# Hybrid decoder trunk: the attention branch by seven products of halves, gated straight from PSUM

## The chip, the cores and the metric

The kernel runs on one core of a Trainium2 chip. TensorE (PE) multiplies matrices into PSUM; VectorE (DVE), ScalarE (ACT) and GpSimd (POOL) work on tiles in the core's memory; SyncE (SP) and POOL issue transfers (DMA). Each engine works through its own instructions in program order, and semaphores make it wait for others. The metric is the device time of one execution in microseconds (us), the median of several.

## The reference

Two layers; each adds a feed-forward block, a mixer of two gated branches, and another feed-forward block to x (512 tokens of 1024 features, f32). What the change touches is in the mixer:

```python
h = rmsnorm(x, ln_mix[l])
z = h @ w_in[l]
u_pool, q, k, v, gate_logits = jnp.split(z, splits, axis=-1)
a = pool_mixer(u_pool, pool_w[l], pool_scale[l]) @ w_pool_branch[l]
...
b = swa_sink_attention(q, k, v, sinks[l]) @ w_attn_branch[l]
g_pool, g_attn = jnp.split(jax.nn.sigmoid(gate_logits), N_BRANCHES, axis=-1)
x = x + (g_pool * a + g_attn * b) @ w_out[l]
```

The attention's output has 512 features (8 heads of 64), both branches' products give 1024, and `w_out` is 1024 x 1024.

## The kernel before

**Products.** Operands are f32 values kept as a high part (a cast by ACT to the type that PE multiplies fast) and a remainder (what DVE subtracts: `lo = src - hi`); a product is three matmuls, high by high, high by remainder, remainder by high. Almost all matrix products go by Winograd's form of Strassen's scheme (`strassen`, line 556): instead of eight products of halves there are seven, named `a11, s1, s2, a12, s3, s4, a22`, whose operands are sums of halves and whose results are added up in PSUM and afterwards. With four blocks of weights, each has up to two chunks of 128x1024 and each chunk takes twelve matmuls of 128x512.

**Weights.** `Weights` (line 178) keeps a plan of chunks in the order of their use. SP loads a chunk into one of seven buffers `raw` (`issue`, line 253); for s1 and s3, whose weights are sums, POOL then issues a transfer that adds the other half onto it (`more`). The sums of s2 and s4 are made by DVE (`add_up`, line 264, into `sums`), or, in blocks called `moved`, that of s4 by one more adding transfer by POOL as soon as the sum of s2 was split (`then`, at the end of `low`). ACT casts the chunk to `wh` (four buffers), DVE takes the remainder `wl` (three). `prep` (line 319), called once per chunk used, does one more step of each; a load waits until the buffer seven chunks earlier has had its last use.

**The mixer** (`mix`, line 920). In the order of PE's program: queries, keys and values; two blocks of gates (`gates`), in whose 28 pieces `side` (line 1150) places the attention, the normalisation and the pooling step by step after tables of slots (`HEADS`, `ATT`, `POOL`); the pool branch (line 1331, `branch` in four quarters of 24 matmuls, with the slots from 28 on beside it); the attention branch, four more quarters, also by `branch`; then the product with `w_out` by the class `Down` (line 597), seven products of two chunks.

The result of a gate is a tile of 128x1024 for each half (i = 0, 1 of the features) and each branch: `z[i]["r"]` and `["u"]` receive the pool branch times its gate (two halves of the tokens, r and u), `z[i]["d"]` and `["p"]` hold the attention's gate. A quarter of the attention branch is evacuated by two DVE operations, the gate times PSUM into `d` or `p`, and that added to `r` or `u`. PE then transposes the four finished tiles (`dn.turned`, eight transposes of 128x128 into the only tile of that kind, `pt`, which ACT and DVE must have emptied before the next group), and from `pt` ACT and DVE make the operands `op` of `Down` and its sums `fa`, `fb`, `fc`. In the rows below `zr_3585` and `zu_3712` are z0's r and u, `zr_4062` and `zu_4204` those of z1; a number is that of the tile.

The attention's output `pv` is written to two tiles per step, `ah` by ACT and `al` by DVE, and the pooling's weights come by one 256 KB transfer `praw`, issued on SP's queue in slot 15 of the gates and split in slot 17.

The first two lines below are the two that decide when a transfer may go and when a weight sum is made; the rest is the evacuation of a quarter of the attention branch.

```python
self.loaded < RAW or self.loads[self.loaded - RAW]["uses"] == 0
if self.summed >= upto + 2 * (c["kind"] == "s2"):
...
nc.vector.tensor_tensor(out=v, in0=pt, in1=v, op=ALU.mult)
add(y, y, v)
```

Of the kernel before, what the change touches and what calls it, by code (L numbers as in the profile page):

```python
# [19 lines left out]
P = 128  # L20
# [95 lines left out]
def trunk(ctx, tc, x0, xT, consts, vecs, rows, w_g4, w_g3, w_d8, w_d6, w_kv, w_uq, w_pool, w_gate, w_br, w_out, out):  # L116
# [61 lines left out]
    class Weights:  # L178
# [3 lines left out]
        def __init__(self):  # L182
# [41 lines left out]
        def block(self, w, sizes, order, start=False, between=(), moved=False):  # L224
# [3 lines left out]
                   "a22": ((1, 1), None), "s2": (None, None), "s4": (None, None)}  # L228
            for k in order:
                for c in range(2):  # L230
# [4 lines left out]
            for c in range(2):  # L235
# [8 lines left out]
            get = lambda *kinds: [name[k, c] for k in kinds for c in range(2)]  # L244
# [311 lines left out]
    def strassen(roles, order, n, sizes, operand, steps, mid={}):  # L556
        A, C, Dd = roles if len(roles) > 2 else (*roles, roles[1])
        bank = {"a11": A, "s2": A, "s3": A, "a22": A, "s1": C, "s4": C, "a12": Dd}
        for kind in order:
            pt, first = bank[kind], kind in ("a11", "s1", "a12") or kind == "s4" and C is Dd  # L560
            k0 = 0
            for c, kn in enumerate(sizes):
                wh, wl = (t[:, :kn * n].rearrange("p (k f) -> p k f", k=kn) for t in W.take(kind))
                for q in range(2):
                    for k in range(kn):
                        ah, al = operand(kind, k0 + k, q)
                        for j, (s, m) in enumerate(((ah, wh), (ah, wl), (al, wh))):
# [10 lines left out]
                if c == 0:  # L578
# [18 lines left out]
    class Down:  # L597


        def __init__(self, turn, op_of, f_of, aside_of, coef, nxt, last=False):  # L600
# [14 lines left out]
            def turned(src, i, t, n):  # L615
# [7 lines left out]
                if i == 0 and t == 1:  # L623
# [24 lines left out]
            def down(n, final, roles, more={}):  # L648
# [71 lines left out]
                }  # L720
                mid.update(more)
# [198 lines left out]
    def mix(ctx, l, nm, nxt):  # L920
# [20 lines left out]
        us = up.tile([P, len(WIN), S], F32, name="us")  # L941
        qT, tiles, parts_, out = {}, {}, {}, {}
# [33 lines left out]

        def pool_weights():
            praw = temp("praw")
# [83 lines left out]
        def attend(b, jp):  # L1062
# [67 lines left out]
            if "ah" not in out:  # L1130
                out.update((t, ap.tile([P, 4, S], F32R, name=t, tag=t)) for t in ("ah", "al"))
# [14 lines left out]
        for g, at in zip(work, [(1, 2), (15, 17), *HEADS, *ATT, *POOL]):  # L1146
            for t in at:
                beside.setdefault(t, []).append(g)

        def side(t):  # L1150
            for g in beside.pop(t, ()):
                next(g)
# [166 lines left out]
        todo = [(i, k) for i in range(2) for k in ("r", "u")] + [(i, k) for i in range(2) for k in ("p", "d")]  # L1319
# [6 lines left out]
        at = 28  # L1326
        for i in range(2):
# [16 lines left out]
        opened(len(todo))  # L1344
        assert not beside, beside
        banks.close()
        order_[:] = order_[1], order_[0], order_[2]
# [7 lines left out]
        def op_of(name):  # L1355
# [4 lines left out]
        spare = up.tile([P, 4, S], F32, name="aside", tag="us")  # L1360
        dn = Down(
            turn, op_of, lambda name: z_tile("f" + name, dict(b="p", a="d", c="u")[name]),
            lambda i: spare[:, 2 * i:2 * i + 2, :], 1.0, nxt,
        )
        for i in range(2):
# [131 lines left out]
```

## Time and profile before

| what | us |
|---|---|
| median of 3 runs (lowest, highest) | 1823.79 (1823.51, 1824.49) |
| the profiled execution in all | 1827.11 |
| its span | 1825.1 |
| busy DVE, ACT in the span | 1512.7, 1133.7 |
| layer 0: attention branch, first to last matmul | 517.59 to 541.14 |

The profiled execution is one more than the three runs, and times of instructions are from it. A row of the timeline reads: start, length, engine, line (here always that of a helper through which every instruction goes, L93 before and L98 after), operation, result <- operands, their sizes; in brackets the idle time of the engine before it and what ended it. Matmuls are pipelined, so the cost of one is the distance of two starts and not its length. A row on waits reads: who waited <- for whom: us in total, times, longest. A row of transfers has the queue, the number, the size and the median time in us from issue to landing.

### The profile page before, as it was taken

What the parts mean: (1) busy time and instruction counts of PE and PEld (TensorE: products, weight loads), DVE (VectorE), ACT (ScalarE), POOL (GpSimd) and SP (SyncE); (2) the same over time, 40 slices, a digit from 0 to 9 for tenths busy, and PEclk for the clock granted to TensorE, in tenths of its full rate; (3) what the DMA queues carried; (4) which work ended last, traced back from release to release, by engine and by line L of the source; (5) the groups of instructions that cost most, each with busy time, mean ns of one, the idle gap of its engine ahead of it and who ended that gap; (6) DMA issues with size and microseconds to landing.
All of it is one profiled execution on the core that took longest, in us unless ns stands there. A gap on an engine that the chain in (4) does not pass through costs nothing.

```text
span 1825.1 us, 24191 instructions
## 1 busy us (share of the span) xinstructions
PE 1815.0 (99%) x8828; PEld 1531.7 (84%) x8828; DVE 1512.7 (83%) x1828; ACT 1133.7 (62%) x1635; POOL 192.5 (11%) x220
## 2 busy tenths in 40 slices
PE   9999999999999999999999999999999999999998
PEld 9988888887788889988888898888867888899887
DVE  8877878889869987887998878788987798878877
ACT  6655555767847754655765555567777477556554
POOL 0100101110001110110100111101100011111000
PEclk9999999999999999999999999999999999999999
DMA  8887867677436867797767779777764368767864
GB/s 258 205 239 182 225 171 188 180 197 192 133 99 160 221 174 193 181 248 181 192 170 205 172 182 235 197 195 177 215 161 123 104 162 207 193 168 193 239 181 127
DMA packets 103831, 338.90 MB, mean 186 GB/s; under 512 B 11264, under 2 KB 11520, under 8 KB 103712
## 3 DMA queue, kind: packets, MB, share of 16 engines
q1 hardware_dynamic: 69408, 231.80, 37.4%
q0 software_dynamic: 34160, 105.53, 33.8%
q8 instruction: 69, 1.13, 0.3%
q14 instruction: 50, 0.41, 0.1%
q10 hardware_dynamic: 144, 0.03, 0.0%
HBM read 320.54 MB, written 2.10 MB: 177 GB/s over the span
## 4 chain that ended last, share of the span: by engine, by line
PE 95%; DVE 3%; ACT 1%; DMA 1%; issue 0%; DVEq 0%; ACTq 0%; SPq 0%
PE mm L93 89%; PE pt L93 3%; DVE wl L93 1%; PE pt_pv L93 1%; PE pt_tp L93 1%; DMA praw<-in_w_pool 1%; DVE more L93 0%; DVE sums L93 0%; ACT wh L93 0%; ACT xg L93 0%; PE cold L93 0%; ACT p L93 0%; DVE xg L93 0%; DVE win L93 0%; DVE m L93 0%
## 5 line engine op out<-in xcount | busy, mean ns | idle before, releaser
L93 PE MATMUL mm<-wh,xg 128*128 128x512 f32 (+2 forms) x2032 | 613.7, 373 | 0.9 <-ACT xg L93 0.8
L93 DVE TENSOR_TENSOR wl<-raw,wh 128x1024 fp32r<-128x1024 f32 (+3 forms) x459 | 524.4, 1148 | 98.1 <-PE mm L93 76.2
L93 ACT CAST wh<-raw 128x1024 fp32r<-128x1024 f32 (+3 forms) x459 | 451.2, 991 | 201.9 <-PE mm L93 122.6
L93 PE MATMUL mm<-wh,more 128*128 128x512 f32 (+1 forms) x1520 | 472.9, 380 | 0.0
L93 PE MATMUL mm<-wh,op 128*128 128x512 f32 x1456 | 465.1, 394 | 0.0
L93 PEld LDWEIGHTS mm<-wh,xg 128*128 128x128 f32 x2032 | 375.4, 188 | 59.0 <-ACT xg L93 2.1
L93 PE MATMUL mm<-wl,xg 128*128 128x512 f32 (+2 forms) x1016 | 376.2, 370 | 0.2 <-DVE wl L93 0.2
L93 PEld LDWEIGHTS mm<-wh,more 128*128 128x128 f32 x1520 | 283.5, 188 | 51.3 <-issue 4.6
L93 PEld LDWEIGHTS mm<-wh,op 128*128 128x128 f32 x1456 | 273.1, 188 | 56.5 <-DVE op L93 1.2
L93 PE MATMUL mm<-wl,more 128*128 128x512 f32 (+1 forms) x760 | 287.5, 378 | 0.1
L93 PE MATMUL mm<-wl,op 128*128 128x512 f32 x728 | 283.6, 390 | 0.0
L93 DVE TENSOR_TENSOR wl<-sums,wh 128x1024 fp32r<-128x1024 f32 (+2 forms) x172 | 197.8, 1151 | 46.3 <-ACT wh L93 29.5
L93 ACT CAST wh<-sums 128x1024 fp32r<-128x1024 f32 (+2 forms) x172 | 169.5, 995 | 79.7 <-DVE sums L93 32.2
L93 PEld LDWEIGHTS mm<-wl,xg 128*128 128x128 f32 x1016 | 191.1, 188 | 27.3 <-DVE wl L93 1.0
L93 PEld LDWEIGHTS mm<-wl,more 128*128 128x128 f32 x760 | 142.9, 188 | 24.1 <-DVE wl L93 1.7
L93 PEld LDWEIGHTS mm<-wl,op 128*128 128x128 f32 x728 | 136.9, 188 | 27.1 <-DVE wl L93 0.3
L93 POOL DMA_DIRECT2D raw<-in_w_g x92 | 78.6, 855 | 714.5 <-DMA raw<-in_w_g 286.9
L93 DVE SCALAR_TENSOR_TENSOR x<-mm,x 128x1024 f32<-128x1024 f32 (+1 forms) x84 | 86.2, 1040 | 13.2 <-PE mm L93 13.0
L93 DVE TENSOR_TENSOR sums<-raw 128x1024 f32<-128x1024 f32 (+1 forms) x86 | 95.4, 1148 | 0.0
L93 ACT CAST op<-fa 128x1024 fp32r<-128x1024 f32 (+1 forms) x42 | 41.6, 991 | 68.7 <-DVE fa L93 68.7
L93 DVE TENSOR_TENSOR sums<-sums,raw 128x1024 f32<-128x1024 f32 (+1 forms) x74 | 84.2, 1138 | 0.0
L93 POOL DMA_DIRECT2D raw<-in_w_d x48 | 40.7, 848 | 388.3 <-DMA raw<-in_w_d 116.4
(253 smaller groups left out, 1672.3 us busy)
## 6 DMA issues: line engine op xcount, KB each, us to landing
raw<-in_w_g SPq DMA_DIRECT2D x160, 512.0 KB, 5.1
raw<-in_w_d SPq DMA_DIRECT2D x100, 512.0 KB, 4.7
raw<-in_w_g POOLq DMA_DIRECT2D x64, 512.0 KB, 6.2
raw<-in_w_g SPq DMA_DIRECT2D x77, 384.0 KB, 4.6
raw<-in_w_d POOLq DMA_DIRECT2D x40, 512.0 KB, 5.6
raw<-in_w_gate SPq DMA_DIRECT2D x40, 512.0 KB, 5.3
raw<-in_w_g POOLq DMA_DIRECT2D x28, 384.0 KB, 5.6
raw<-in_w_uq SPq DMA_DIRECT2D x20, 512.0 KB, 4.3
```

Source lines behind the costliest of these rows:

```text
L93: return lambda *args, **kw: self.tc.keep_in_program_order(call(*args, **kw))
```

## The change

The attention's output stays one f32 tile `o`, copied by ACT. From it come the operands of seven products (`forms`): seven casts by ACT and eleven DVE operations of 128x512, in the slots 28 to 39 (`FORMS`), beside the pool branch and the first attention products. The attention branch itself is now `gated`, a `strassen` with one chunk per product: seven times twelve matmuls. Its weights are a block of seven chunks instead of four.

In the scheme the result of a product belongs to up to four quarters; here each product is multiplied by a gate directly from PSUM, as a partial result, and added: seven DVE evacuations, of which three go to tiles of their own (`va` twice, `vb`) and four over the gate. Two sums are made by DVE; five are transfers by POOL that add onto `zr` or `zu` (`gather`). The evacuation of a22 is put off (`rest`) to a place behind the first chunk's first half of w_out's a11.

`Down` takes `early=True`: the transposes come in the order `z0.r` (inside s4 of the attention), `z0.u` and `z1.u` (inside the first and second chunk of w_out's a11), `z1.r` (behind its s1), and `fa` is an ACT copy of the first transposed tile from which the second is subtracted. The block of `w_out` is `moved`: its s4 sums are POOL transfers rather than DVE operations. In moved blocks the s2 sums are made one step before their use, no longer two steps sooner. The pooling weights get a tile of their own, and their transfer is issued in slot 4, split in slot 16; all slots of attention and pooling move by one or so.

SP's queue, the mixer of layer 0 from the gates on (rows of before, then of the change; `in_w_...` are the weights):

```order
L93 DMA raw<-in_w_gate 128x1024 x20
L93 DMA raw<-in_w_br 128x1024
L93 DMA praw<-in_w_pool 128x512
L93 DMA raw<-in_w_br 128x1024 x7
L93 DMA raw<-in_w_out 128x1024 x10
```

```order
L98 DMA raw<-in_w_gate 128x1024 x12
L98 DMA praw<-in_w_pool 128x512
L98 DMA raw<-in_w_gate 128x1024 x8
L98 DMA raw<-in_w_br 128x1024 x9
L98 DMA raw<-in_w_out 128x1024 x10
```

The pooling weights stand nine loads further ahead, and there is one more load of `w_br`.

POOL's transfers from the last of the gates to the second feed-forward block, before:

```order
L93 DMA sums_3947<-in_w_gate 128x1024
L93 DMA raw_4476<-in_w_out 128x1024
L93 DMA raw_4509<-in_w_out 128x1024
L93 DMA raw_4731<-in_w_out 128x1024
L93 DMA raw_4841<-in_w_out 128x1024
L93 DMA x_83<-aside_4688 128x2x512 x2
```

and with the change (here `zr_3585` and `zu_3722` are z0's r and u, `zr_4078` and `zu_4227` z1's):

```order
L98 DMA raw_4578<-in_w_out 128x1024
L98 DMA zr_3585<-va_4710 128x1024
L98 DMA zu_4227<-va_4710 128x1024
L98 DMA zu_3722<-vb_4711 128x1024
L98 DMA raw_4788<-in_w_out 128x1024
L98 DMA zu_4227<-zp_4144 128x1024
L98 DMA raw_4858<-in_w_out 128x1024
L98 DMA zr_4078<-zd_4505 128x1024
L98 DMA sums_4854<-in_w_out 128x1024
L98 DMA x_83<-aside_4697 128x2x512
```

Five gathers stand among the weight transfers, the last two each behind one of the s3 weights of `w_out`.

DVE, end of the attention branch and start of `Down`, before:

```order
L93 TENSOR_TENSOR zp_3654<-mm0_4684,zp_3654 128x1024
L93 TENSOR_TENSOR zu_3712<-zu_3712,zp_3654 128x1024
L93 TENSOR_TENSOR wl_4727<-raw_4439,wh_4666 128x1024
L93 TENSOR_TENSOR zd_3985<-mm2_4686,zd_3985 128x1024
L93 TENSOR_TENSOR zr_3585<-zr_3585,zd_3985 128x1024
L93 TENSOR_TENSOR wl_4758<-raw_4575,wh_4729 128x1024
L93 TENSOR_TENSOR fa_4784<-pt_4687,fb_4754 128x1024
L93 TENSOR_TENSOR op_4782<-pt_4687,op_4782 128x1024
```

and with the change, from the remainder of the last attention weights:

```order
L98 TENSOR_TENSOR wl_4784<-raw_4483,wh_4767 128x1024
L98 SCALAR_TENSOR_TENSOR zp_4144<-mm0_4693,zp_4144 128x1024
L98 TENSOR_TENSOR wl_4805<-raw_4665,wh_4786 128x1024
L98 TENSOR_TENSOR op_4823<-pt_4696,op_4823 128x1024
L98 TENSOR_TENSOR zp_3665<-mm2_4695,zp_3665 128x1024
L98 TENSOR_TENSOR zu_3722<-zu_3722,zp_3665 128x1024
L98 TENSOR_TENSOR wl_4836<-raw_4667,wh_4807 128x1024
L98 TENSOR_TENSOR wl_4852<-raw_4511,wh_4838 128x1024
L98 TENSOR_TENSOR sums_4854<-raw_4665,raw_4511 128x1024
L98 TENSOR_TENSOR fa_4825<-fa_4825,pt_4696 128x1024
L98 SCALAR_TENSOR_TENSOR zd_4505<-mm0_4693,zd_4505 128x1024
```

The evacuation `zd_4505` that the last gather waits for stands behind the first s2 sum of `w_out` and behind `fa`.

PE behind `Down`'s s1, with the change; the transposes here are those of `z1.r`, the tile that the last gather completes:

```order
L98 MATMUL mm2_4695<-wl_4889,op_4878 128x512
L98 MATMUL mm2_4695<-wh_4856,op_4878 128x512
L98 MATMUL pt_4696<-cst_79,zr_4078 128x128 x8
L98 MATMUL mm1_4694<-wh_4893,op_4918 128x512
L98 MATMUL mm1_4694<-wl_4927,op_4918 128x512
```

The diff, cut to its core:

```diff
-START = 3
-HEADS = ((-2, 0, 0), (1, 4, 4), (6, 10, 10), (10, 13, 13))
-ATT = tuple(tuple(START + 3 * n + d for d in (0, 1, 2, 3, 4, 5, 6, 7, 9, 10, 11)) for n in range(8))
-POOL = ((2, 3, 16, 18, 19, 20, 21), (9, 12, 20, 21, 22, 23, 24), (15, 18, 20, 23, 25, 26, 27), (20, 21, 22, 24, 26, 27, 27))
+START = 2
+HEADS = ((-2, 0, 0), (1, 3, 3), (6, 9, 9), (9, 12, 12))
+ATT = tuple(tuple(START + 3 * n + d for d in (0, 1, 2, 3, 4, 5, 6, 7, 9, 10)) for n in range(8))
+POOL = ((2, 4, 15, 17, 18, 20, 21), (8, 11, 18, 20, 21, 22, 23), (14, 17, 20, 23, 24, 25, 26), (19, 20, 22, 24, 25, 26, 27))
+FORMS = dict(
+    h_s4=28, l_s4=29, h_a11=31, l_a11=31, s1=32, h_s1=32, l_s1=33, s3=33, h_s3=33, h_a12=34, s2=34, l_s3=34, h_s2=34,
+    l_a12=34, l_s2=35, a22=37, h_a22=38, l_a22=39,
+)
...
-                        for side in range(2):
-                            for i in range(2):
-                                for c in range(2):
-                                    self.add("br", CH, w_br[l, side, i, c])
-                        self.block(lambda h, k, c, w=w_out[l]: w[h, 2 * k + c], (CH, CH), ORDER)
+                        for i in range(2):
+                            for c in range(2):
+                                self.add("br", CH, w_br[l, 0, i, c])
+                        self.block(lambda h, k, c, w=w_br[l, 1]: w[h, k], (CH,), ORDER)
+                        self.block(lambda h, k, c, w=w_out[l]: w[h, 2 * k + c], (CH, CH), ORDER, moved=True)
...
-                if self.summed >= upto + 2 * (c["kind"] == "s2"):
+                if self.summed >= upto + 2 * (c["kind"] == "s2" and "then" not in c):
...
-                if i == 0 and t == 1:
+                if early and i == t == 0:
+                    high("a11", pt, n)
+                    f["a"] = f_of("a")[:, :, :n]
+                    nc.scalar.copy(out=f["a"], in_=pt)
+                elif early and i == 0:
+                    f["b"] = f_of("b")[:, :, :n]
+                    nc.scalar.copy(out=f["b"], in_=pt)
+                    nc.vector.tensor_tensor(out=f["a"], in0=f["a"], in1=pt, op=ALU.subtract)
+                    high("s1", f["a"], n)
+                elif i == 0 and t == 1:
...
-                    return flush
+                    return None if early else flush
...
+                if early:
+                    mid.update({("s1", 0, 1): gathered, ("s1", 1, 1): flush, ("s2", 0, 0): lambda: low("a12")})
...
+        def forms(src, put):
+            view = lambda k, t: src[:, 2 * k:2 * k + 2, t * HT:(t + 1) * HT]
+            b11, b12, b21, b22 = view(0, 0), view(0, 1), view(1, 0), view(1, 1)
+            at = dict(a11=b11, s2=b11, s3=b12, a12=b21, a22=b21, s4=b22)
+            made = {}
+            def high(kind):
+                made[kind] = [t.rearrange("p (k t) -> p k t", k=2) for t in put(kind)]
+                nc.scalar.copy(out=made[kind][0], in_=at[kind])
+            def low(kind):
+                hi, lo = made[kind]
+                nc.vector.tensor_tensor(out=lo, in0=at[kind], in1=hi.bitcast(F32), op=ALU.subtract)
+            def s1():
+                at["s1"] = temp("d").rearrange("p (k t) -> p k t", k=2)
+                nc.vector.tensor_tensor(out=at["s1"], in0=b11, in1=b12, op=ALU.subtract)
+            def s3():
+                nc.vector.tensor_tensor(out=b12, in0=b22, in1=b12, op=ALU.subtract)
+            def minus(t, other):
+                nc.vector.scalar_tensor_tensor(out=t, in0=t, scalar=-1.0, in1=other, op0=ALU.mult, op1=ALU.subtract)
+            steps = dict(s1=s1, s3=s3, s2=lambda: minus(b11, b12), a22=lambda: minus(b21, b11))
+            for kind in ORDER:
+                steps["h_" + kind] = lambda kind=kind: high(kind)
+                steps["l_" + kind] = lambda kind=kind: low(kind)
+            return made, steps
         def pool_weights():
...
-            praw = temp("praw")
+            praw = mp.tile([P, S], F32, name="praw")
...
-            o = pv[:, :2 * P].rearrange("p (j t) -> p j t", j=2)
-            nc.scalar.copy(out=out["ah"][:, js, sl], in_=o)
-            yield
-            nc.vector.tensor_tensor(
-                out=out["al"][:, js, sl], in0=o, in1=out["ah"][:, js, sl].bitcast(F32), op=ALU.subtract
-            )
+            if not out:
+                out.append(ap.tile([P, 4, S], F32, name="o", tag="al"))
+            nc.scalar.copy(out=out[0][:, js, sl], in_=pv[:, :2 * P].rearrange("p (j t) -> p j t", j=2))
...
-        for g, at in zip(work, [(1, 2), (15, 17), *HEADS, *ATT, *POOL]):
+        for g, at in zip(work, [(1, 2), (4, 16), *HEADS, *ATT, *POOL]):
...
+        def times(out, pt, gate, minus):
+            if not minus:
+                nc.vector.tensor_tensor(out=out, in0=pt, in1=gate, op=ALU.mult)
+            else:
+                nc.vector.scalar_tensor_tensor(
+                    out=out, in0=pt, scalar=-1.0, in1=gate, op0=ALU.mult, op1=ALU.mult
+                )
+        def gather(y, v):
+            nc.gpsimd.dma_start(out=y, in_=v, accum_op=ALU.add)
+        HOME = dict(a11=(0, "r"), s1=(1, "u"), s2=(0, "u"), a12=(0, "r"), s3=(1, "u"), s4=(0, "u"), a22=(1, "r"))
+        GATE = dict(r="d", u="p")
+        rest = []
+        def gated(roles, at, made, mid):
+            def step(kind, n):
+                i, k = HOME[kind]
+                y, gate = z[i][k], z[i][GATE[k]]
+                def go(pt):
+                    if kind == "a22":
+                        rest.append(lambda: evacuate(pt))
+                    else:
+                        evacuate(pt)
+                    side(at + n)
+                def evacuate(pt):
+                    if kind in ("a11", "s1", "s2"):
+                        times(aside(kind), pt, gate, i)
+                        gather(y, aside(kind))
+                        opened(1)
+                        return
+                    times(gate, pt, gate, i)
+                    if i:
+                        gather(y, gate)
+                    else:
+                        nc.vector.tensor_tensor(out=y, in0=y, in1=gate, op=ALU.add)
+                return go
+            strassen(
+                roles, ORDER, S, (2,), lambda kind, k, q: [t[:, k, q * P:(q + 1) * P] for t in made[kind]],
+                {kind: step(kind, n) for n, kind in enumerate(ORDER)}, mid,
+            )
...
-        todo = [(i, k) for i in range(2) for k in ("r", "u")] + [(i, k) for i in range(2) for k in ("p", "d")]
+        todo = [(i, k) for i in range(2) for k in ("r", "u")] + [(0, "d"), (1, "p"), (0, "p"), (1, "d")]
...
-        for i in range(2):
-            w = [W.take("br") for _ in range(2)]
-            for t in (1, 0):
-                pt = roles[2 if t else 1]
-                def between(i=i, t=t):
-                    if i and t:
-                        dn.turned(z[0]["r"], 0, 0, S)
-                        dn.low("a11")
-                    if not t:
-                        W.prep()
-                branch(i, t, pt, [(out["ah"][:, k, :], out["al"][:, k, :]) for k in range(4)], w, between)
-                y, v = z[i]["ru"[t]], z[i]["dp"[t]]
-                if (i, t) == (0, 0):
-                    dn.turned(z[0]["u"], 0, 1, S)
-                nc.vector.tensor_tensor(out=v, in0=pt, in1=v, op=ALU.mult)
-                add(y, y, v)
-                if not t:
-                    W.prep()
+        gated(
+            roles, 36, attended,
+            {("s4", 0, 0): lambda: dn.turned(z[0]["r"], 0, 0, S),
+             ("s4", 0, 1): lambda: dn.low("a11")},
+        )
...
-        dn.down(S, True, roles, {("a11", 0, 0): lambda: dn.low("s1"), ("a11", 0, 1): lambda: dn.turned(z[1]["u"], 1, 1, S)})
+        dn.down(S, True, roles, {
+            ("a11", 0, 0): lambda: [dn.turned(z[0]["u"], 0, 1, S), rest.pop()()], ("a11", 0, 1): lambda: dn.low("s1"),
+            ("a11", 1, 0): lambda: dn.turned(z[1]["u"], 1, 1, S), ("a11", 1, 1): lambda: dn.low("s2"),
+        })
 
```

More of the change, by code (lines that the diff above doesn't have):

```diff
@@ L228, in block @@
                    "a22": ((1, 1), None), "s2": (None, None), "s4": (None, None)}
+            chunks = range(len(sizes))
             for k in order:
-                for c in range(2):
+                for c in chunks:
                     s, m = (None if p is None else w(*p, c) for p in src[k])
@@ L234, in block @@
                     others = [self.add(kind, CH, part) for kind, part in between]
-            for c in range(2):
+            for c in chunks:
                 name["s2", c]["of"] = name["a11", c], name["s1", c]
@@ L243, in block @@
             loads = ("a11", "s1") if start else ("s1", "a11")
-            get = lambda *kinds: [name[k, c] for k in kinds for c in range(2)]
+            get = lambda *kinds: [name[k, c] for k in kinds for c in chunks]
             self.loads[first:] = [*get(loads[0]), *others, *get(loads[1], "a12", "s3", "a22")]
@@ L577, in strassen @@
                 k0 += kn
-                if c == 0:
+                if c < len(sizes) - 1:
                     W.prep()
@@ L597, in trunk, with __init__ @@
     class Down:
-        def __init__(self, turn, op_of, f_of, aside_of, coef, nxt, last=False):
+        def __init__(self, turn, op_of, f_of, aside_of, coef, nxt, last=False, early=False):
             f, ops, turns = {}, {}, []
@@ L940, in mix @@
         step_v = mp.tile([P, NB - 1, HKV, HD], F32, name="step_v")
-        us = up.tile([P, len(WIN), S], F32, name="us")
-        qT, tiles, parts_, out = {}, {}, {}, {}
+        us = up.tile([P, len(WIN), S], F32, name="us", tag="us")
+        qT, tiles, parts_, out = {}, {}, {}, []
         qs = lambda b: tiles["q"][:, b, :].rearrange("p (h d) -> p h d", h=HQ)
@@ L1145, in mix, with scheduled, put_attn @@
         beside = {}
-        for g, at in zip(work, [(1, 2), (15, 17), *HEADS, *ATT, *POOL]):
+        for g, at in zip(work, [(1, 2), (4, 16), *HEADS, *ATT, *POOL]):
             for t in at:
-                beside.setdefault(t, []).append(g)
+                beside.setdefault(t, []).append(lambda g=g: next(g))
         def side(t):
-            for g in beside.pop(t, ()):
-                next(g)
+            for f in beside.pop(t, ()):
+                f()
+        def scheduled(made_steps, slots):
+            made, steps = made_steps
+            for k, t in slots.items():
+                beside.setdefault(t, []).append(steps[k])
+            return made
+        def put_attn(kind):
+            if kind == "a11":
+                tiles["ah"] = ap.tile([P, 4, S], F32R, name="ah", tag="ah")
+            if kind in ("a11", "s1"):
+                return [tiles["ah"][:, 2 * (kind == "s1") + i, :] for i in range(2)]
+            if kind in ("a12", "s2"):
+                if "over" not in tiles:
+                    tiles["over"] = up.tile([P, 4, S], F32R, name="over", tag="us")
+                return [tiles["over"][:, 2 * (kind == "s2") + i, :] for i in range(2)]
+            at = dict(s4=(2, 0), s3=(2, 1), a22=(0, 0))[kind]
+            return [nm.place(side, *at) for side in range(2)]
         operand = lambda kind, k, q: [t[:, q * P:(q + 1) * P] for t in nm.of(OF[kind], k)]
@@ L1310, in branch, with aside @@
                     between()
+        spare = {}
+        def aside(kind):
+            if not spare:
+                both = xl.tile([P, 8, HT], F32, name="va", tag="b21")
+                flat = lambda t: t.rearrange("p (q a) t -> p q (a t)", q=2)
+                spare.update(a11=flat(both[:, :4, :]), s1=flat(both[:, 4:, :]))
+                spare["s2"] = flat(xl.tile([P, 4, HT], F32, name="vb", tag="b111"))
+            return spare[kind]
+        def times(out, pt, gate, minus):
[36 more added lines that the diff above has]
+            )
         left_over = queries()
@@ L1326, in mix @@
         at = 28
+        attended = scheduled(forms(out[0], put_attn), FORMS)
         for i in range(2):
@@ L1343, in mix @@
                 at += 2
-        opened(len(todo))
-        assert not beside, beside
         banks.close()
-        order_[:] = order_[1], order_[0], order_[2]
+        order_[:] = order_[2], order_[0], order_[1]
         pf = ctx.enter_context(tc.tile_pool(name="pf", bufs=1, space=PSUM, reuse_waits="tile"))
```

9 lines of the change are left out of this document (4 added, 5 removed).

## The prediction

> **What bounds the kernel now.** I read the page's busy line first, then the chain that ended last, then what PE waited for.
>
> ```profile
> span 1825.1 us, 24191 instructions
> PE 1815.0 (99%) x8828; PEld 1531.7 (84%) x8828; DVE 1512.7 (83%) x1828; ACT 1133.7 (62%) x1635; POOL 192.5 (11%) x220
> PE 95%; DVE 3%; ACT 1%; DMA 1%; issue 0%; DVEq 0%; ACTq 0%; SPq 0%
> PE pt_pv L93 <- DVE al L93: 3.2, 1, 3.2
> PE cold L93 <- DVE warm_in L93: 1.1, 1, 1.1
> PE mm L93 <- ACT xg L93: 0.8, 3, 0.3
> PE mm L93 <- DVE wl L93: 0.2, 1, 0.2
> ```
>
> PE is busy for 99% of the span, the chain lies on it for 95%, and its waits sum to some 5 us, one of them 3.2. So the kernel is as long as its list of matmuls, and a shorter list pays one for one, but only where DVE (83% on average) and the transfers can follow. That must be read in the stage that changes: the end of the pool branch, the attention branch, and the w_out product.
>
> ```profile
> 500.00:517.60 17.60, 17.60 (x84) 13.22 (x84) 7.01 (x8) 6.25 (x9) 0.00 (x0) 1.00 0.37 97
> 517.60:541.10 23.50, 23.50 (x113) 19.67 (x112) 16.74 (x15) 12.11 (x15) 0.85 (x1) 1.00 0.33 86
> 580.00:601.90 21.90, 21.64 (x102) 17.26 (x100) 19.57 (x29) 16.79 (x30) 2.46 (x3) 1.00 0.54 143
> ```
>
> These rows of the windows view (length, then busy PE, PEld, DVE, ACT, POOL, then clock, DMA share, GB/s) are layer 0: the second half of the pool branch, the attention branch, and the start of the second feed-forward block. PE is full. DVE has 10.6 us free in the first, 6.8 in the second, 2.3 in the third.
>
> **PE's saving.** The change takes 96 matmuls of 128x512 of each attention branch down to 84 and adds none elsewhere.
>
> ```profile
> 517.59 0.39 PE L93 MATMUL mm<-wh,ah 128*128 128x512 f32 x1
> 528.24 0.39 PE L93 MATMUL mm<-wh,al 128*128 128x512 f32 x1
> 528.47 1.03 PE L93 MATMUL pt<-cst,zu 128*128 128x128 f32 x8
> 529.26 0.48 PE L93 MATMUL mm<-wh,ah 128*128 128x512 f32 x1
> 529.58 0.40 PE L93 MATMUL mm<-wl,ah 128*128 128x512 f32 x1
> 541.14 0.39 PE L93 MATMUL mm<-wh,op 128*128 128x512 f32 x1
> ```
>
> The first two are the first and the 48th matmul of the branch: (528.24-517.59)/47 = 0.2267 us apart. Twelve fewer are **-2.72 us per layer**. A group of eight transposes takes 0.88 (528.47 to 529.58 less one pitch); there are four such groups before and after, so they cancel. The old branch with one group inside runs from 517.59 to 541.14.
>
> **The pool weights.** In layer 1 PE stood for 3.20 us behind this transfer, and the clock paid more.
>
> ```profile
> 344.26 1.40 PE mm L93 x6
> 601.93 22.06 PE mm L93 x96
> 1249.13 1.40 PE mm L93 x6
> 1350.03 11.23 DMA praw<-in_w_pool
> 1510.69 22.33 PE mm L93 x96
> 1363.01 0.65 PE L93 MATMUL pt_pv<-p,qkv 128*64 128x256 f32 x4 [3.20 <-DVE al L93]
> 1349.77 1.13 PE L93 MATMUL mm<-qkv 64*128 64x256 f32 x8
> 1364.03 2.08 PE L93 MATMUL mm<-qkv 64*128 64x256 f32 x8
> ```
>
> The same two pieces of the chain lie 601.93-344.26 = 257.67 apart in layer 0 and 1510.69-1249.13 = 261.56 in layer 1. The difference, 3.89, is the 3.20 of waiting plus 0.69 of slower matmuls behind it (the same eight take 2.08 instead of 1.13). The change issues this transfer eleven slots earlier; a slot holds about twelve matmuls, so that is some 11 x 2.72 = 30 us for a landing that was about 3 us late. The wait goes: **-3.9**, and nothing takes its place, since the gate weights behind it on SP's queue are used only after several slots. The profiled execution took 1827.11 in all (span plus 2.0), the median of the runs is 1823.79. 1827.11-3.89 = 1823.22 is close to the median, so I take it that the timed runs mostly had no such wait, and that this term brings the forecast back to the median rather than below it.
>
> [...]
>
> **DVE and ACT in the attention branch.** Per layer DVE gets three more weight remainders `wl`, one more operation on results (7 evacuations and 2 sums instead of 4 and 4) and 11 operations of 128x512 on `o`, and loses 8 small `al` ones: with the pitches below 4 x 1.135 + 11 x 0.60 = 11.1 us less eight that are each shorter than 0.60, so 6 to 11 us more; two sums of `w_br` are matched by two of `w_out` that become transfers. ACT gets about as much. ACT had 11.4 us free in 517.6 to 541.1 and casts in front of DVE, so I cost it at nothing.
>
> ```profile
> 560.60 1.22 DVE L93 TENSOR_TENSOR wl<-raw,wh 128x1024 fp32r<-128x1024 f32 x1
> 561.73 1.22 DVE L93 TENSOR_TENSOR sums<-sums,raw 128x1024 f32<-128x1024 f32 x1
> 570.81 0.68 DVE L93 TENSOR_TENSOR xg<-more,xg 128x512 fp32r<-128x512 f32 x1
> 571.41 1.21 DVE L93 SCALAR_TENSOR_TENSOR x<-mm,x 128x1024 f32<-128x1024 f32 x1
> 523.30 1.23 DVE L93 TENSOR_TENSOR zp<-mm,zp 128x1024 f32<-128x1024 f32 x1 [2.99 <-PE mm L93]
> 524.56 1.23 DVE L93 TENSOR_TENSOR zu<-zu,zp 128x1024 f32<-128x1024 f32 x1
> ```
>
> Starts are 1.135 apart for 128x1024 (two rounds 1.13 and 1.14), 0.60 for 128x512, and 1.26 where the second needs the first. I set t = 0 at the first attention matmul and lay out the new order. PE without waits: products begin at 0, 2.72, 5.44, 8.16, 10.88, 13.60 (with the transposes of `z0.r` inside) and 17.20; w_out's a11 at 19.92, with the transposes of `z0.u` in its first chunk and those of `z1.u` due at 24.88 in its second; s1 from 27.12; the transposes of `z1.r` due at 32.56. DVE, in order from 0.13, without a pause: up to `wl_4784` twelve wide operations, three of 128x512 and 0.26 of dependence, so 0.13 + 13.62 + 1.80 + 0.26 = **15.8**; up to `sums_4854` eight more wide and 0.13, **25.0**; then `fa - pt`, the operand that empties the one transpose tile, **26.1**; then the postponed evacuation of a22, **27.3**. So even with free transfers the transposes of `z1.u`, due at 24.88, stand 1.2 for DVE, and `wl_4927`, 8 operations behind, is at 35.0 for a matmul due at 33.67: **1.4 late** from DVE alone.
>
> **The gathers.** This is the term that decides. Five 512 KB sums per layer now go by POOL's queue, in program order with two transfers of w_out's weights (`raw_4788`, `raw_4858`), each of which adds onto a load that SP can only issue when DVE has freed a buffer.
>
> ```profile
> raw<-in_w_out SPq DMA_DIRECT2D x10, 512.0 KB, 3.4
> raw<-in_w_out POOLq DMA_DIRECT2D x4, 512.0 KB, 5.5
> raw<-in_w_out POOLq DMA_DIRECT2D x1, 512.0 KB, 6.5
> raw<-in_w_out POOLq DMA_DIRECT2D x1, 512.0 KB, 7.3
> 545.20 0.84 POOL L93 DMA_DIRECT2D raw<-in_w_out  x1 [13.65 <-PE pt L93]
> x<-aside POOLq DMA_DIRECT2D x1, 512.0 KB, 5.0
> 773.75 0.85 POOL L93 DMA_DIRECT2D raw<-in_w_g  x1 [3.52 <-ACT wh L93]
> 774.29 1.53 POOL L93 DMA_DIRECT2D x<-p  x1
> raw<-in_w_g POOLq DMA_DIRECT2D x1, 512.0 KB, 5.3
> x<-p POOLq DMA_DIRECT2D x1, 512.0 KB, 7.3
> ```
>
> A load lands after 3.4, a weight sum on POOL after 5.5 (four in layer 1) to 7.3, that at 545.20 after 6.5; a sum onto `x` alone after 5.0, but issued 0.54 behind another after 7.3: it lands (774.29+7.3)-(773.75+5.3) = 2.5 behind the one in front of it. For the new kernel I take the row of two together.
> - `zu_4227<-zp`: `raw_4788` is loaded at 15.8+0.1, lands 19.3; its POOL sum takes 5.5 (to 24.8); the gather behind it lands at 27.3. Due at 24.88: PE waits **2.4**, and DVE's 26.1 lies inside it.
> - `zr_4078<-zd`: `raw_4858` is loaded at 25.0+0.1, lands 28.5; its sum takes 6.5 (to 35.0, much the place of the 545.20 row: t = 27.6 there); the gather lands at 37.5. Due at 32.56: late by **4.9** in all, 2.5 more than the first wait.
>
> Lower bound: every gather lands 5.0 behind its own issue (19.9+5.0 = 24.9, no wait; 28.5+0.5+5.0 = 34.0, 1.4 late), so 1.4 in all, the same as from DVE alone. Upper bound: sums of 7.3 for both: 19.3+7.3+2.5 = 29.1, so 4.2 at the first, and 28.5+7.3+2.5 = 38.3, so 5.7 in all, plus 0.7 where a wait passes 3.2. Below 1.4 only if DVE's row pitch fell, which no row shows. I take 4.9, from the row of two POOL transfers together, which is what this order makes.
>
> [...]
>
> **Sum.** Per layer -2.72 + 4.9 - 0.26 (the missing PE time in the window 580 to 601.9, which a delayed PE gives DVE time to cover) = +1.9. Two layers +3.8. 1827.11 - 3.89 + 3.8 = **1827.0**, against the median 1823.79 +0.18%.
>
> Costed at nothing: the ten more transfers of 512 KB per layer (DMA share 0.33 to 0.54 in these windows; uncovered, they lengthen landings, as in the upper bound); the sums s2 of the gates and of w_out that DVE now makes one step before their use (in the gates DVE has pauses; in w_out PE's waits cover it, else the 1.4); the shifted slots of attention and pooling (if a chain there gets tight, tenths at each).
>
> **Rivals.**
> - **The gathers stay hidden**: sums overlap in the queue, as the 5.0 alone suggests, and only DVE's 1.4 is left, or nothing. 2 x (-2.72-0.26+1.4) = -3.2: 1823.22-3.2 = 1820.1; with nothing left 1817.3. For it: `z` lies in the chip as `x` does, and the data are small beside a DMA share of a third. Against: the 2.5 between two sums in a row.
> - **Slower, by the clock**: the weight sum in front of each gather takes 7.3 or more because SP's loads run beside it, the first wait passes 3.2 and PE pays 0.7 behind each. From a wait of 2.72+0.26 per layer the change loses. 2 x (5.7+0.7-2.98) = +6.8: 1830.1; with both waits above 3.2, 1831.5. For it: the 7.3 row; against: the median 5.5.
> - **The timed runs had the praw wait too**, and the profiled one was long for another reason. Then 1823.79-3.89+3.8 = 1823.7. For it: it would need only the same queue on each run; against: the 1823.2 above.
> That the change doesn't do what it says is out: the order has 84 matmuls in place of 96.
>
> **Chances.** Forecast 0.42 (its own range 1825.1 to 1828.7, from waits of 3.9 per layer, with 5.5 for the last weight sum too, to 5.7), hidden 0.20, slower by the clock 0.20, praw in all runs 0.18. 0.2% is 3.6 us, about what a measurement of this kernel can tell from none: 1820.1 and 1827.4. The forecast lies near that edge: 0.24 same, 0.18 slower. Hidden: 0.17 faster, 0.03 same. Clock: slower. Praw: 0.15 same, 0.03 faster. So faster 0.20, same 0.42, slower 0.38. The range goes from inside the hidden case, 1819.5, to both waits with their clock, 1831.5.
>
> **What would show it.** In the new profile: PE with 24 matmuls fewer; no wait of `pt_pv` for the pool weights; per layer a wait of the transposes into `pt` of 2 to 3 us at `z1.u` and of 1.5 to 4 at `z1.r`, released by the gathers' DMAs; on POOL the weight sums ahead of `zu<-zp` and `zr<-zd`. If these waits are absent or end with DVE's `fa`, the first rival holds; if the matmuls behind them are slow, the second. I am wrong if DVE's backlog shows as waits for `wl` in the second feed-forward block, which I cost at nothing.

## The result, and the profile after

The change is slower: 1844.88 us median (1842.11 to 1848.1) against 1823.65 (1822.82 to 1824.49), a ratio of 1.0112 (95% interval 1.0095 to 1.0128). The profiled execution took 1843.11, its span 1841.3, with 24247 instructions. The page's busy line and its shares of the chain:

```profile
PE 1817.8 (99%) x8804; PEld 1530.9 (83%) x8804; DVE 1530.5 (83%) x1842; ACT 1147.9 (62%) x1657; POOL 207.8 (11%) x238
PE 85%; DVE 6%; DMA 6%; ACT 2%; issue 1%; SPq 0%; POOL 0%; DVEq 0%; POOLq 0%; ACTq 0%
```

What PE waited for (us in total, times, longest):

```profile
PE pt L98 <- DMA zr<-zd: 6.9, 2, 3.5
PE pt L98 <- DMA zu<-zp: 5.8, 2, 3.3
PE mm L98 <- DVE x L98: 1.9, 2, 1.0
PE mm L98 <- DVE wl L98: 1.8, 6, 0.4
```

PE has 24 matmuls fewer and yet 2.8 us more of busy time; the chain has gone from 95% on PE to 85%. The two waits that the prediction named are there, in both layers, and the one for the pool weights is gone. The windows view gives each layer from its first attention matmul to the same piece of the second feed-forward block, of the kernel before (layer 0; layer 1 is 84.34 long too, with PE busy for 84.06) and of the changed one (both layers):

```profile
517.59:601.93 84.34, 84.05 (x401) 69.27 (x399) 73.23 (x77) 56.67 (x86) 8.30 (x9) 1.00 0.60 154
```

```profile
518.26:612.35 94.09, 85.42 (x390) 68.98 (x388) 78.33 (x83) 61.28 (x91) 14.07 (x16) 0.96 0.74 183
1433.29:1527.25 93.96, 86.33 (x390) 69.92 (x388) 78.10 (x83) 61.28 (x91) 13.67 (x15) 0.95 0.74 183
```

The loss lies here: 9.75 + 9.62 = 19.4 us. Taken apart, the matmuls saved are -5.4, PE's idle time is 8.67 + 7.63 instead of 0.29 + 0.28, so +15.7, and the busy time that is left is 9.1 longer than the saving allows: most of it is matmuls that run slower behind the waits. The four large waits on PE's timeline:

```profile
547.08 1.29 PE L98 MATMUL pt<-cst,zu 128*128 128x128 f32 x8 [3.28 <-DMA zu<-zp]
560.16 1.07 PE L98 MATMUL pt<-cst,zr 128*128 128x128 f32 x8 [3.55 <-DMA zr<-zd]
1461.31 1.06 PE L98 MATMUL pt<-cst,zu 128*128 128x128 f32 x8 [2.48 <-DMA zu<-zp]
1474.17 1.94 PE L98 MATMUL pt<-cst,zr 128*128 128x128 f32 x8 [3.37 <-DMA zr<-zd]
```

and the windows directly behind each (the clock is the column after POOL):

```profile
547.00:551.00 4.00, 3.92 (x15) 3.37 (x16) 3.26 (x3) 1.30 (x2) 1.72 (x2) 0.60 0.79 244
560.00:566.00 6.00, 5.83 (x23) 4.83 (x24) 1.79 (x2) 4.17 (x5) 0.00 (x0) 0.72 1.09 249
1461.30:1467.30 6.00, 6.00 (x24) 4.95 (x25) 4.89 (x5) 3.27 (x5) 1.73 (x2) 0.72 0.73 176
1474.10:1480.10 6.00, 5.93 (x19) 5.10 (x20) 1.22 (x1) 3.83 (x4) 0.00 (x0) 0.54 1.08 248
```

4 x 0.40 + 6 x 0.28 + 6 x 0.28 + 6 x 0.46 = 7.7 us of full clock are missing there, 1.6 to 2.8 behind each wait. Why the gathers are late is read from POOL's timeline:

```profile
538.94 0.85 POOL L98 DMA_DIRECT2D raw<-in_w_out  x1 [8.96 <-DVE zp L98]
539.48 1.19 POOL L98 DMA_DIRECT2D zu<-zp  x1
549.17 0.85 POOL L98 DMA_DIRECT2D raw<-in_w_out  x1 [8.50 <-DVE sums L98]
549.91 0.99 POOL L98 DMA_DIRECT2D zr<-zd  x1
570.78 0.86 POOL L98 DMA_DIRECT2D raw<-in_w_g  x1 [13.09 <-DVE wl L98]
571.32 1.54 POOL L98 DMA_DIRECT2D x<-aside  x1
```

(the first two long brackets name DVE, but `zp` had ended 3.7 us and `sums` 5.9 us before; what came last is taken to be the other condition of these transfers, SP's load) and from the landings of two transfers issued in 540 to 560, the weight sum of 549.17 and the gather behind it:

```profile
raw<-in_w_out POOLq DMA_DIRECT2D x1, 512.0 KB, 8.4
zr<-zd POOLq DMA_DIRECT2D x1, 512.0 KB, 10.1
```

DVE's timeline has the sum that frees the buffer for that load:

```profile
542.08 1.22 DVE L98 TENSOR_TENSOR sums<-raw 128x1024 f32<-128x1024 f32 x1
```

`sums_4854` ends at 543.2 (the next start), t = 25.0 as laid out; the load that follows it lands 5.9 later instead of 3.5, its weight sum goes at 549.17, the gather 0.74 behind it, and lands after 10.1, at t = 41.8 instead of 37.5. A third pair of the same kind had no term in the prediction: the sum onto x, `x<-aside`, behind the first weight sum of the next block.

### The profile page after: what moved, and what is told of

Read it like the earlier page. It is cut to its first block, busy times and chain, and to the rows that moved or that the text cites. A ratio compares the mean times of both kernels' runs of the same rounds, so it can differ in the third digit from the quotient of the medians.

```text
span 1841.3 us, 24247 instructions
## 1 busy us (share of the span) xinstructions
PE 1817.8 (99%) x8804; PEld 1530.9 (83%) x8804; DVE 1530.5 (83%) x1842; ACT 1147.9 (62%) x1657; POOL 207.8 (11%) x238
## 4 chain that ended last, share of the span: by engine, by line
PE 85%; DVE 6%; DMA 6%; ACT 2%; issue 1%; SPq 0%; POOL 0%; DVEq 0%; POOLq 0%; ACTq 0%
PE mm L98 80%; PE pt L98 3%; DVE wl L98 2%; DMA sums<-in_w_uq 1%; DMA x<-aside 1%; DMA zr<-zd 1%; PE pt_pv L98 1%; ACT wh L98 1%; PE pt_tp L98 1%; DMA raw<-in_w_g 1%; DVE more L98 1%; DVE x L98 0%; ACT xg L98 0%; DVE sums L98 0%; DMA zu<-zp 0%
## 5 line engine op out<-in xcount | busy, mean ns | idle before, releaser
L98 PE MATMUL mm<-wh,more 128*128 128x512 f32 (+1 forms) x1568 | 486.7, 380 | 0.0
L98 PE MATMUL mm<-wh,op 128*128 128x512 f32 x1456 | 470.5, 398 | 0.0
L98 PEld LDWEIGHTS mm<-wh,more 128*128 128x128 f32 x1568 | 292.2, 188 | 52.4 <-issue 2.9
L98 PE MATMUL mm<-wl,more 128*128 128x512 f32 (+1 forms) x784 | 296.7, 378 | 0.8 <-DVE wl L98 0.8
L98 DVE TENSOR_TENSOR wl<-sums,wh 128x1024 fp32r<-128x1024 f32 (+1 forms) x176 | 202.8, 1154 | 45.9 <-ACT wh L98 29.4
L98 ACT CAST wh<-sums 128x1024 fp32r<-128x1024 f32 (+1 forms) x176 | 173.8, 996 | 82.1 <-DVE sums L98 30.3
L98 PEld LDWEIGHTS mm<-wl,more 128*128 128x128 f32 x784 | 147.3, 188 | 25.7 <-DVE wl L98 2.6
L98 DVE TENSOR_TENSOR sums<-raw 128x1024 f32<-128x1024 f32 (+2 forms) x88 | 98.5, 1154 | 0.0
L98 DVE TENSOR_TENSOR sums<-sums,raw 128x1024 f32<-128x1024 f32 (+2 forms) x72 | 81.9, 1138 | 0.0
```

Source lines behind the costliest of these rows:

```text
L98: return lambda *args, **kw: self.tc.keep_in_program_order(call(*args, **kw))
```

## The experiments

"The change" below is the changed kernel; each ratio is to the kernel before, timed beside it (median 1823.6 to 1824.3).

### more_behind: the two weight sums behind the gathers

```diff
             if c["more"] is not None:
-                nc.gpsimd.dma_start(out=c["raw"]..., in_=c["more"], accum_op=ALU.add)
+                go = lambda: nc.gpsimd.dma_start(out=c["raw"]..., in_=c["more"], accum_op=ALU.add)
+                go() if self.held is None else self.held.append(go)
...
             nc.gpsimd.dma_start(out=y, in_=v, accum_op=ALU.add)
+            while W.held:
+                W.held.pop(0)()
```

> The changed kernel with one thing moved: the two s3 weight sums of w_out on POOL's queue stand behind the gathers zu<-zp and zr<-zd instead of ahead of them; all else, the number of transfers too, is as in the change. Theory A (order on POOL's queue: a gather is late because the weight sum in front of it waits for its load): both gathers are issued as soon as their data are there (t = 17 and 27.4), land 5 to 7.5 later; of the waits 3.3 and 3.5 us there remain about 1.2 (DVE's fa) and 0 to 1, without slow matmuls behind them; time 1823 to 1828. Theory B (the 16 DMA engines are full there, share 0.96 to 1.09): a gather still takes some 10 us, so the wait at z1.r stays at 3 us or more with its slow clock, and the time is above 1833.

1833.08 us, ratio 1.0049 (1.0034 to 1.0064): 11.8 under the change, with no transfer and no instruction fewer. The landing of the last gather:

```profile
zr<-zd POOLq DMA_DIRECT2D x1, 512.0 KB, 4.6
```

PE's waits:

```profile
PE mm L98 <- DVE x L98: 6.8, 3, 3.0
PE mm L98 <- DVE wl L98: 3.4, 5, 2.3
PE pt L98 <- DVE fa L98: 1.4, 2, 0.7
```

and POOL's timeline, the gather and then the place where the second wait comes from:

```profile
547.26 0.84 POOL L98 DMA_DIRECT2D zr<-zd  x1 [7.21 <-DVE zd L98]
...
569.56 0.85 POOL L98 DMA_DIRECT2D raw<-in_w_g  x1 [10.96 <-DMA raw<-in_w_g]
570.10 1.53 POOL L98 DMA_DIRECT2D x<-aside  x1
```

The share of the DMA engines while this gather is under way, here and in the change:

```profile
547.26:551.86 4.60, 4.60 (x22) 3.78 (x21) 4.31 (x4) 1.76 (x3) 1.69 (x2) 1.00 1.04 248
```

```profile
549.91:560.03 10.12, 6.71 (x27) 5.11 (x25) 6.62 (x6) 3.97 (x4) 3.98 (x5) 0.94 0.99 225
```

The gather lands in 4.6 us instead of 10.1, though the 16 engines are as full (share 1.04 and 0.99): theory A holds for these two gathers, B falls. The time misses A's 1823 to 1828, because a second wait has grown: for x, whose sum was issued 0.54 behind a weight sum that waited 10.96 for its load. Of the 3.4 for `wl`, 2.28 is one wait at 384.44, early in layer 0's mixer and ahead of everything that this edit moves (there it is 0.64 in x_ahead, 2.29 in no_gathers and 2.44 in dve_sums; in the change none over 0.2 stands between 345 and 518). The code up to there is the same, so some 2 us of this execution are not due to the edit; why the wait differs is open.

### no_gathers and dve_sums: what DVE alone costs

```diff
-            nc.gpsimd.dma_start(out=y, in_=v, accum_op=ALU.add)
+            pass          # no_gathers
+            nc.vector.tensor_tensor(out=y, in0=y, in1=v, op=ALU.add)   # dve_sums
```

> The changed kernel with the five gathers per layer left out, so five partial results are missing from the gated sum; 10 transfers fewer, no instruction more. Theory A and B (gathers, by order or by their load): no wait of PE for a transfer at the transposes; what remains is DVE: fa at t = 26.1 for transposes due at 24.88, 1.2 to 1.4 us per layer; time about 1820 to 1822. Theory C (DVE's added work is what makes PE late, and the gathers only end last): waits for fa, op and wl take the place of the gathers', some 3 us or more per layer with slow matmuls; time above 1828.

> The changed kernel with the five gathers per layer as DVE additions at the same places: 10 transfers fewer, 5 x 1.13 us more on a DVE that is busy without a pause from t = 0 to 30. Theory C (DVE is the bound there): DVE stands 4 to 6 us later at fa and zd than in the change, PE waits that much, the clock drops, and the time is 1840 or more. Theory A and B: DVE's delay is partly taken up by PE's own due times (zr is needed only at t = 32.6) and the weights' lead; about 1828 to 1836, under the change in any case.

no_gathers 1834.56, ratio 1.0056 (1.0041 to 1.0071); dve_sums 1847.77, 1.0129 (1.0111 to 1.0147). PE's waits of no_gathers:

```profile
PE mm L98 <- DVE x L98: 7.2, 2, 4.6
```

and one of dve_sums:

```profile
PE mm L98 <- DVE vb L98: 4.2, 2, 2.1
```

With the gathers gone the same wait for x stands there as in more_behind, so those five transfers are not what delays it. I had expected 1820 to 1822 by A and waits for fa, op and wl by C; both missed the wait for x (fa has 0.7 per layer, as in more_behind). Some 2 us of its time are the wait of 2.29 early in layer 0's mixer. dve_sums shows the other edge: DVE additions in place of the transfers are no cheaper than the transfers with their waits (1.0129 against 1.0112, intervals that overlap). Its time is in C's range and above A's and B's 1828 to 1836, but C had not the whole cause: PE waits 6.8 for x there too, and 2.4 for wl early in layer 0's mixer. What is due to DVE are the waits of 4.2 for `vb`, 2.4 for `zu`, 1.4 for `fa` and 1.2 for `op`.

### early_praw: the pool weights alone

```diff
-            praw = temp("praw")
+            praw = mp.tile([P, S], F32, name="praw")
...
-        for g, at in zip(work, [(1, 2), (15, 17), *HEADS, *ATT, *POOL]):
+        for g, at in zip(work, [(1, 2), (4, 17), *HEADS, *ATT, *POOL]):
```

> The kernel before with the pool weights in a tile of their own and their transfer in slot 4 instead of 15, nothing else. If the timed runs have no wait for these weights (as 1827.11-3.89 = 1823.2 suggests): within 1 us of the kernel before, 1823 to 1824.5, and a profile without a wait of pt_pv. If they have it each time: 1819.5 to 1820.5.

1822.65 us (10 runs), ratio 0.9990 (0.9979 to 1.0001), and no wait of `pt_pv` in its profile (span 1820.8 instead of 1825.1). So the wait was mostly one of the profiled execution, as the prediction took it: the timed runs differ by 0.9 us, which these runs can't tell from none, and the -3.9 of a wait in every run (0.9979) lies at the edge of the interval.

### x_ahead: the next pair turned as well

The list `held` of more_behind is now kept until the second `x<-aside` has been issued.

> The kernel more_behind with one more pair turned on POOL's queue: the first weight sum of the second feed-forward block stands behind the second x<-aside instead of ahead of it. Theory A (order on POOL's queue also makes the second wait: in more_behind x<-aside was issued at 570.10, 0.54 us behind that weight sum, which waited for its load): x<-aside is issued some 10 us earlier, PE's waits for DVE x (6.8 us over both layers in more_behind) go to under 0.5, and the time falls by 6 to 9 us to 1824 to 1827; DVE's 0.7 to 0.9 per layer at the transposes and the waits for wl (3.4) stay. Theory C (DVE's backlog is what makes PE late there): the wait only changes its name to wl or op, and the time stays above 1830.

1826.45 us (11 runs), ratio 1.0018 (1.0009 to 1.0026), 6.6 under more_behind. PE's waits:

```profile
PE mm L98 <- DVE wl L98: 2.0, 6, 0.6
PE mm L98 <- DVE x L98: 1.4, 2, 0.8
PE pt L98 <- DVE fa L98: 1.4, 2, 0.7
```

and a row of its chain, the second sum onto x (start, us, what):

```profile
558.89 14.56 DMA x<-aside
```

As A said but for a rest: `x<-aside` is issued at 558.89 instead of 570.10, and yet PE waits 0.6 and 0.8 for x. The sum took 14.56 us to land, behind two s4 weight sums and the first x sum on the same queue. By order alone, 18.4 of the change's 21.2 us are undone. (Of what x_ahead gains on more_behind in the profiles, 1.6 belong to the wait at 384.)

### late_sums, own_sums, sums_behind, both: the rest

```diff
-                if self.summed >= upto + 2 * (c["kind"] == "s2" and "then" not in c):
+                if self.summed >= upto + (2 if "then" not in c else -1) * (c["kind"] == "s2"):   # late_sums
...
-        self.block(..., w=w_out[l]: ..., (CH, CH), ORDER, moved=True)
+        self.block(..., w=w_out[l]: ..., (CH, CH), ORDER)          # own_sums
...
-            ("a11", 0, 0): lambda: [dn.turned(z[0]["u"], 0, 1, S), rest.pop()()],
+            ("a11", 0, 0): lambda: [dn.turned(z[0]["u"], 0, 1, S), rest.pop()(), summed()],   # sums_behind, both
```

In sums_behind the sums that `prep` would make behind a22 are left to `summed`. `both` has that and own_sums' second edit, with the s2 sums at x_ahead's place.

> The kernel x_ahead with the s2 sums of moved blocks one more step later (now in the step of their cast), so that DVE makes fa and the evacuation zd before the first s2 sum of w_out. Theory C' (the rest of the loss is DVE's order around t = 25): the waits at z0.u and z1.u (0.9 per layer) fall to 0.3 or less, and the time is 1 to 2 us under x_ahead. Rival: the cast and the remainder of s2 then come too late, here or in the gates, and waits for wl of 0.5 to 1 us per layer take their place: the time is equal to x_ahead or up to 3 us above it.

> The kernel x_ahead with w_out's block no longer moved: its two s4 sums are DVE operations again (2 x 1.13 us per layer), 4 POOL transfers of 512 KB fewer in all; the s2 sums return to two steps sooner, so that one more of them stands ahead of fa. Theory C (DVE is the scarce engine in this stretch): PE waits 1.1 us more per layer at fa and some more behind it, 2 to 6 us slower than x_ahead. Theory B (traffic is scarce): landings get shorter and the time is equal to x_ahead or below it.

> The kernel x_ahead with the first s2 sum of w_out moved on DVE from ahead of fa to behind the evacuation zd, its cast on ACT left where it was (late_sums had pulled sum and cast into one step, and ACT waited). Theory C' (what is left at the transposes of z1.u is DVE's order): PE's wait for fa (0.7 per layer) goes and zr's gather starts 1.1 us sooner; 1 to 2 us under x_ahead, 1824 to 1825.5. Rival: DVE is full up to t = 45 in any order, so the wait turns up again at op or wl: equal to x_ahead.

> As sums_behind, and w_out's two s4 sums by DVE as in own_sums, without that kernel's second s2 sum ahead of fa. Theory (both of what is left is known: own_sums had no wait for x but 1.8 per layer at fa, x_ahead 0.7 at each): no wait for x, under 0.2 per layer at fa, waits for wl as before (2 us in all); 2 to 3 us under x_ahead, 1823.5 to 1824.5, so no faster than the kernel before by more than a measurement can tell. Rival: the two added DVE sums per layer, in a stretch where DVE is 85 to 95% busy, come back as 1 us or more of waits for wl: equal to x_ahead or slower.

| kernel | us | ratio to before (95%) |
|---|---|---|
| late_sums | 1858.85 | 1.0190 (1.0176 to 1.0204) |
| own_sums | 1826.97 | 1.0020 (1.0009 to 1.0031) |
| sums_behind | 1834.44 | 1.0050 (1.0037 to 1.0063) |
| both | 1825.25 | 1.0006 (0.9998 to 1.0015) |

PE's largest wait in late_sums:

```profile
PE mm L98 <- ACT aside L98: 11.3, 2, 5.7
```

in own_sums:

```profile
PE pt L98 <- DVE fa L98: 3.6, 2, 1.8
```

and in sums_behind, on PE's timeline:

```profile
574.42 1.12 PE L98 MATMUL mm<-cst,x 128*128 128x128 f32 x4 [4.87 <-DVE x L98]
```

with what POOL had issued before it:

```profile
556.64 0.86 POOL L98 DMA_DIRECT2D sums<-in_w_out  x1 [8.87 <-ACT wh L98]
557.18 1.53 POOL L98 DMA_DIRECT2D x<-aside  x1
557.90 1.75 POOL L98 DMA_DIRECT2D raw<-in_w_out  x1
558.47 2.06 POOL L98 DMA_DIRECT2D sums<-in_w_out  x1
560.36 1.40 POOL L98 DMA_DIRECT2D x<-aside  x1
```

late_sums missed both of its cases: a sum in the step of its own cast makes ACT wait for DVE (3.64 us at 556.70 and again at 564.64), and what is queued behind that cast on ACT is the copy `aside` that empties a PSUM tile for PE. own_sums has no wait for x any more and 1.1 more per layer at fa, as C said, but not C's 2 to 6 us: the sums onto x land after 5.6 us (median of two) instead of 11.7, as B said, and the two cancel: equal to x_ahead. sums_behind was to gain 1 to 2 us and lost 8 (its wait for fa is gone, but wl has 4.0 and x 8.5): one DVE operation moved makes a load later, its weight sum slips behind the first x sum, and the second x sum then stands behind four transfers. It is the same trap for a third time. `both`, with two of those transfers gone, has waits of 0.9 at most (its row for wl is 2.6 in 7 waits); it is not distinguishable from the kernel before and no faster, as expected of it, though 1825.25 is above the 1823.5 to 1824.5 that I gave and its waits for wl are longer than the 2.0 of x_ahead, as the rival said. None of these versions is faster than the kernel before.

## Why the prediction was wrong

- **The saving**: 24 matmuls are gone, and nothing took their place on PE. Right.
- **DVE's layout**: `wl_4784` was to end at 15.8 and ended at 534.0 - 518.26 = 15.8; `sums_4854` at 25.0, measured 25.0. Right. The 1.4 that it gave as the loss from DVE alone is near what more_behind and x_ahead show at `fa` and `zu` (0.9 per layer), but not the whole of the cost without large waits: in `both` a layer still takes 84.56 where 84.34 less 2.72 = 81.62 was to be had.

```profile
518.64:603.20 84.56, 83.02 (x389) 66.59 (x387) 79.90 (x85) 60.86 (x91) 11.86 (x13) 1.00 0.77 189
```

  Of these 2.9 us, 1.25 are idle time of PE (waits for wl, op, x, zu and `aside` of 0.2 to 0.4). The other 1.7 are longer busy time at a granted clock of 1.00, which no row puts down to anything; a matmul is drawn 0.39 long at a pitch of 0.227, so a gap of less than 0.16 between two would not show as idle.
- **The failed step, the waits at z1.u and z1.r** (the term "4.9"): place, releaser and order in the queue were as said. The size failed: at z1.r PE stood at 560.16 - 518.26 = 41.9 instead of 32.56, 9.3 late (8.3 in layer 1). At the first gather only the load was longer, 4.9 instead of 3.5; sum and gather took 8.0, as forecast. At the second the load behind `sums_4854` took 5.9 instead of 3.5, and sum and gather behind it 10.9 instead of 9.0. I priced each transfer by rows in which the queue held it and one other; here SP's loads and POOL's sums ran together on full engines (the window 540 to 547 has a share of 0.98). That this is what made the load and the sum longer is likely and not shown: no run changes the share alone.
- **The clock**: costed at nothing in the forecast, since waits of 2.4 and 2.5 were under the 3.2 row, and at 0.7 per wait in the rival. No run shows that a wait has to pass 3.2 us before the clock costs anything, as the rival had it: the cost was 1.6 to 2.8 behind each of four waits, and one of 2.48 had it too (0.72 over 6 us). Behind the first wait of a layer it is inside the 9.3, since the landing of the second gather, and not PE, sets the time at z1.r; behind the second, 1.7 and 2.8 come on top. The 0.7 was itself read wrongly: it is what is left of 3.89, a difference to layer 0, whose part up to the first attention matmul is itself 0.96 longer than in early_praw (173.33 and 172.37). The sixteen small matmuls from this `pt_pv` on and the twelve of 128x512 behind them tell it directly in the profile before, in layer 0 without a wait and in layer 1 behind the 3.20 (the row at 1363.01 in the prediction):

```profile
455.81 0.65 PE L93 MATMUL pt_pv<-p,qkv 128*64 128x256 f32 x4
460.76 0.39 PE L93 MATMUL pt_tp<-dh,w_pool 128*128 128x512 f32 x1
1369.52 0.39 PE L93 MATMUL pt_tp<-dh,w_pool 128*128 128x512 f32 x1
```

  460.76 - 455.81 = 4.95, and 1369.52 - 1363.01 = 6.51: 1.56 more. "Slower, by the clock" was the nearest case, but its 1830.1 to 1831.5 is too small, by this price and by the landings; its condition, a weight sum of 7.3 or more, held for the second sum (8.4) and not for the first (5.5).
- **A term left out**: the order of POOL's queue also changed at the end, where `x<-aside` fell behind `raw<-in_w_g`. The changed order showed it, but I read that queue only up to the last gather. In the change it costs PE only 1.9, since PE is late already; as soon as the gathers are in time it costs 6.8 (more_behind).
- **The -0.26**: PE was to win back its idle 0.26 at the end of the stretch. It didn't: the same wait for `xg`, 0.27, stands at 601.93 before and at 612.35 with the change.
- **The pool weights**: -3.9 in the profiled execution (4.8 by early_praw's layer 1, 177.22 to 172.38), next to nothing in the runs. Right in the forecast of the runs.

With these terms a layer comes out: 9.3 late at z1.r, 1.7 of clock behind it, 1.0 for x, 0.4 for wl, less 2.7, is 9.7, measured 9.75; in layer 1 it is 8.3 + 2.8 + 0.9 + 0.4 - 2.7 = 9.7, measured 9.62. The forecast had 4.9 - 0.26 - 2.72 = 1.9.

What is shown: order on POOL's queue is 18.4 of the 21.2 us. What stays open: whether the rest can be brought under the 5.4 us that the matmuls save. Part of that rest is not in this stretch. From the piece at which the prediction compared the layers (1249.13 in the profile before) to the first attention matmul, early_praw (the kernel before with the early pool weights alone) and the change take:

```profile
1249.57:1421.95 172.38, 172.38 (x884) 137.65 (x882) 145.22 (x267) 125.23 (x245) 15.38 (x18) 1.00 0.63 169
```

```profile
1259.62:1433.29 173.67, 173.09 (x883) 137.42 (x882) 148.91 (x269) 127.85 (x251) 17.07 (x20) 1.00 0.67 173
```

That is 1.3 us more (1.0 in layer 0; in `both` 1.1 and 0.8). The moved slots, the later s2 sums and the operands of the seven products lie there, which the prediction costed at nothing; which of them it is, no run shows.

## What to carry to other kernels

On POOL's queue a data transfer was as late as the prefetch ahead of it: the gather of 549.91 went 0.74 us behind a weight sum for which POOL had stood 8.50, and landed after 10.1 instead of the 4.6 of more_behind. So when a data transfer is put where prefetches are issued, list for the whole queue, to the end of the stage, what each entry waits for, and put what the critical engine needs ahead of what only fills a buffer. A wait that is added to a full TensorE can cost more than its length (here 1.6 to 2.8 us more), so a saving of 2.7 us doesn't cover two waits that look like 2.5 each. And where work moves from TensorE to an engine that is 94% busy, as DVE is in `both`, the saving can go without any single wait that stands out.

## What the runs showed of the hardware that was not expected

- The granted clock fell behind a wait of 2.48 us (0.72 over 6 us) and not behind one of 2.66 in more_behind (1.00 in 579.20 to 583.20): the length of the wait alone didn't decide here. Two waits of dve_sums say the same, one of 2.12 that ends at 533.70, with a clock of 0.50 in the row behind it, and one of 2.11 that ends at 1450.77, with 1.00:

```profile
530.97:534.38 3.41, 1.29 (x6) 0.79 (x5) 3.38 (x4) 2.51 (x3) 0.00 (x0) 1.00 0.28 82
534.38:537.79 3.41, 3.41 (x10) 2.63 (x9) 3.38 (x4) 0.00 (x0) 0.00 (x0) 0.50 0.20 80
1449.15:1452.56 3.41, 1.79 (x8) 1.49 (x9) 3.38 (x4) 1.84 (x2) 0.00 (x0) 1.00 0.45 154
1452.56:1455.97 3.41, 2.99 (x16) 2.22 (x15) 3.38 (x4) 1.05 (x1) 0.00 (x0) 1.00 0.00 0
```

  In the profile of the change the windows view gives 0.50 for 3.41 us from 547.78, from 561.43 and from 1462.55, and for 6.83 us from 1472.79; half of 3.41 is the 1.6 to 1.7 us of full clock that are missing behind the first three of its four waits. Why one wait of 2 to 3 us has it and another has not, no run shows.
- Sums of 512 KB on POOL's queue landed after 4.6 us (more_behind's `zr<-zd`) with none just ahead, after 7.5 and 10.1 behind one other (the change's `zu<-zp` and `zr<-zd`) and after 14.56 behind three (x_ahead), with SP's loads running beside them (their queue has 32.1% of the 16 engines in 540 to 560 of the change, 34.0% in 545 to 585 of more_behind and 33.2% in 554 to 560 of x_ahead).
